# Hybrid encoder layer on one core: prompt's attention output stored in DRAM, sample's w_out low parts on VectorE, norms spread through the first MLP's end, two projection chunks multiplied beside each other

## The chip, the cores and the metric

One core of a Trainium2 chip runs the whole kernel. The metric is the device time of one execution in microseconds; less is better. The kernel before has a median of 1564.66 us over 3 runs (1561.09 to 1566.85).

Five engines work beside each other: TensorE (PE in the profile, with PEld for its weight loads), VectorE (DVE), ScalarE (ACT), GpSimd (POOL) and SyncE (SP), which here issues the transfers between DRAM and the on-chip memory. Matmul results land in eight banks of 128 x 512 fp32, which DVE and ACT read.

## The reference, cut to what matters

Two requests go through the same layer with the same weights: prompt (512 rows) and sample (1024 rows), each of width 1024.

```
h = RMSNorm(x);  z = h @ w_in                   # q 512, k 128, v 128, ca 512, cb 512 columns
A = windowed attention(q, k, v): 8 heads, 2 kv heads, |q-k| <= 128, bias per head, sink logit
B = ca * sigmoid(cb) -> depthwise conv over 31 rows -> LayerNorm over the 512 channels -> silu
x = x + concat(A, B) @ w_out
u = depthwise conv over 3 rows (RMSNorm(x) @ w_up)      # 2 x 2816 columns
x = x + (silu(u[:, :2816]) * u[:, 2816:]) @ w_down
y = RMSNorm(x)
```

All is fp32. Nearly every product is made of three matmuls on operands that are split in two: the high part (`hi`, a cast to the type fp32r, on ACT) and the low part (`lo` = value - hi, a subtraction on POOL or DVE); hi*hi, hi*lo and lo*hi are summed in a bank.

## The kernel before

**Stages.** Rows come in blocks of 128 (prompt 4, sample 8) and in groups of 512 (`nt` 0 for prompt, 1 and 2 for sample). The work goes in this order:

1. *Front.* Prompt's four x tiles are loaded and normed (`norm_in_place`, L241: sum of squares on ACT for even tiles and on DVE for odd ones, then `rstd_of`, L175, with two POOL instructions: scale and EPS at L176, power -0.5 at L177; scaling on DVE, L250). `transposed` (L254) turns them on TensorE into eight pieces of 128 x 512; ACT writes the high part (L260), DVE the low one (L261).
2. *Projection of prompt.* w_in comes in chunks of 128 columns (`order`, 14 for prompt: cb and ca of four channel groups, then k, v and four q; then the same in another order for sample). `want_raw` loads a chunk two ahead, `want_w` splits it one ahead (`split`, L189: cast L192 on ACT, subtraction L193 on POOL, or on DVE if asked). `step` (L445) multiplies one chunk with one group of rows and evacuates the bank. For the first two chunks `proj` makes the products with the weight's low part last. `constants` loads and turns small vectors after the first chunk.
3. *Projection of sample, with prompt's rest at its side.* While sample's chunks are multiplied (the loop behind `side.append(prompt())`), the generator `prompt` is advanced beside them: attention of its eight units (block x kv head), with the norm of the conv branch (`conv_norm`, L678) of a block behind each of the last four units; then, for each half n of w_out's columns, its eight pieces are loaded and split, and four out halves are made (`out_half`, L716: 24 matmuls, residual add L731, and after the second half the sum of squares L737 and its root). Then `make_h2` scales the rows and turns them for the MLP.
4. *First MLP (prompt), 22 steps, with sample's rest at its side* (`ffn_step`; L299 to L302 are the matmuls of `proj`; the three taps of the MLP's conv are L856 on ACT and L852 on DVE). From step U0 = 2 the generator `sample` gives attention for 16 units, then the 16 pieces of w_out, each loaded WOA = 5 pieces ahead and split (all low parts on POOL, since DW2 = 0), then what is left of the conv taps, and NE = 2 conv norms. The rest of sample's norms and out halves follows between this MLP and the next.
5. *Second MLP (sample)*, in an order written out by hand on TensorE, and the down projection of all rows, then `finish` (L1466) block by block: squares on ACT L1471, POOL L1472, L1473 and the power L1474, scaling on DVE L1484, store.

**What sets the order.** Within a stage the program's order is a list of generators. `tick` (L277), called every few matmuls, advances the queues by credits: `rate` for `side` (RA, RB, RBO, RD, RN, RE by stage), `conv` and `late` for the conv taps of prompt and sample (`convs`, `late`; CA, CB, CL, CLO, CD). A conv of one channel group is 31 taps; most are DVE's L354 on a bank, the last NOFF are a scaling on ACT and an add on POOL. `behind` places each tap's priority BACK places later for the scheduler, which then settles each engine's instruction order from the dependences and these priorities. Each engine and each queue works through its own list in order; SP's list holds all loads and stores.

**Buffers.** SBUF slots are taken and freed by name of size (q 4096 bytes, h 2048, c, d, s); a tile gives its slot back when the last reference goes. Banks: a (3), u (2), b (2), c (1); `use` says which job may take which. Sample's attention output (two tiles of 4 x 128 per block, high and low part) goes to DRAM (`catd`, 8 blocks, L661) and is loaded back in `load_cat` (L673). Prompt's stays on the chip from `values` until `out_half`.

## Time and profile before

| | us |
|---|---|
| median of 3 runs | 1564.66 (1561.09 to 1566.85) |
| profiled execution, its own time | 1561.29 |
| span of its trace | 1559.5 |
| PE busy | 1505.8 (97%) |
| DVE busy | 1126.9 (72%) |
| ACT busy | 795.2 (51%) |
| POOL busy | 709.7 (46%) |
| mean granted TensorE clock | 0.99 |
| matmuls and transposes in the trace | 6843 |

The profile shows one execution. Its page gives busy time of each engine, the span in 40 equal slices (39 us each; a digit is tenths of the slice), DMA queues, the chain that ended last, and groups of instructions by line. A busy PE is not PE at its peak: matmul ends are modelled, and at a lower granted clock the same matmul counts for longer. Further views used: busy time of each engine in chosen stretches, the list of what an engine waited for, the timeline, and the groups with shapes kept apart (shape out<-in, count | busy, mean ns of one | idle time ahead and what ended it).

### The profile page before, as it was taken

How to read it: one execution, taken by the hardware profiler on the slowest of the kernel's cores; microseconds unless marked ns; L12 is line 12 of the kernel's file. 1: busy time of each engine (PE TensorE's matmuls, PEld its weight loads, DVE VectorE, ACT ScalarE, POOL GpSimd, SP SyncE). 2: the span in 40 equal slices, each digit the busy share in tenths (PEclk: the TensorE clock that was granted, in tenths of full speed). 3: DMA queues.
4: the chain of work that ended last, by engine and by line, in shares of the span. 5: the costliest groups of instructions: out<-in, count | busy, mean ns of one | idle time of the engine just before them, and what ended most of it. 6: DMA issues, size and time to landing. Idle time of an engine off the chain costs nothing. (4 is left out here: it accounts for less than half of the span.)

```text
span 1559.5 us, 20112 instructions
## 1 busy us (share of the span) xinstructions
PE 1505.8 (97%) x6843; PEld 1228.9 (79%) x6843; DVE 1126.9 (72%) x1604; ACT 795.2 (51%) x1404; POOL 709.7 (46%) x566
## 2 busy tenths in 40 slices
PE   8998998899999999899999999999999999999997
PEld 6787787787888888777777888888888788888885
DVE  7999767858789785334868777777776845569883
ACT  4634654335787786623455445554545543444354
POOL 6652343226666775947434555555544000003355
PEclk9999999899999999999999999999999999999999
DMA  7582334447344346779332333333332582357644
GB/s 229 157 212 78 108 99 124 128 131 226 111 132 130 117 130 182 241 235 305 108 95 75 102 101 102 102 102 102 102 115 75 191 280 82 105 166 233 220 132 162
DMA packets 228780, 227.17 MB, mean 146 GB/s; under 512 B 13268, under 2 KB 168348, under 8 KB 228549
## 3 DMA queue, kind: packets, MB, share of 16 engines
q1 hardware_dynamic: 228677, 225.88, 45.6%
q8 instruction: 54, 0.88, 0.2%
q14 instruction: 49, 0.40, 0.1%
HBM read 164.74 MB, written 62.14 MB: 145 GB/s over the span
## 5 line engine op out<-in xcount | busy, mean ns | idle before, releaser
L193 POOL TENSOR_TENSOR q<-q,q 128x1024 fp32r<-128x1024 f32 x72 | 173.3, 2414 | 93.5 <-ACT q L192 36.7
L955 POOL TENSOR_TENSOR q<-q,q 128x512 fp32r<-128x512 f32 x101 | 140.7, 1398 | 163.8 <-ACT q L1065 151.5
L955 DVE TENSOR_TENSOR h<-h,h 128x512 fp32r<-128x512 f32 (+2 forms) x202 | 158.4, 817 | 66.2 <-ACT h L959 26.1
L1413 PE MATMUL w<-h,h 128*128 128x512 f32 x462 | 181.4, 393 | 0.5 <-DVE q L1200 0.5
L1414 PE MATMUL w<-h,h 128*128 128x512 f32 x462 | 181.5, 393 | 0.0
L1415 PE MATMUL w<-h,h 128*128 128x512 f32 x462 | 181.1, 392 | 0.0
L1079 PE MATMUL w<-h,q 128*128 128x512 f32 x448 | 176.4, 394 | 3.0 <-ACT w L1171 1.6
L1081 PE MATMUL w<-h,q 128*128 128x512 f32 x448 | 175.5, 392 | 1.0 <-POOL q L955 1.0
L1080 PE MATMUL w<-h,q 128*128 128x512 f32 x426 | 166.5, 391 | 0.0
L299 PE MATMUL u<-h,q 128*128 128x512 f32 x400 | 161.1, 403 | 5.0 <-DVE h L852 4.2
L300 PE MATMUL u<-h,q 128*128 128x512 f32 x400 | 158.9, 398 | 0.0
L302 PE MATMUL u<-h,q 128*128 128x512 f32 x384 | 152.2, 396 | 2.7 <-POOL q L193 2.7
L952 POOL TENSOR_TENSOR q<-q,q 128x1024 f32<-128x1024 f32 x12 | 33.1, 2769 | 238.1 <-DMA h<-gb 197.4
L354 DVE SCALAR_TENSOR_TENSOR c<-c,cvw,c 128x512 f32<-128x512 f32 x184 | 137.9, 750 | 2.9
L959 ACT CAST h<-h 128x512 fp32r<-128x512 f32 x120 | 71.8, 619 | 95.9 <-DVE h L955 42.5
L299 PE MATMUL b<-h,q 128*128 128x512 f32 x256 | 102.3, 400 | 2.7 <-DVE d L384 1.9
L1413 PEld LDWEIGHTS w<-h,h 128*128 128x128 f32 x462 | 86.8, 188 | 20.7 <-ACT h L959 0.9
L1415 PEld LDWEIGHTS w<-h,h 128*128 128x128 f32 x462 | 86.7, 188 | 19.7
L852 DVE SCALAR_TENSOR_TENSOR h<-u,fw,h 128x511 f32<-128x511 f32 x88 | 65.4, 744 | 50.8 <-ACT h L856 50.1
L1414 PEld LDWEIGHTS w<-h,h 128*128 128x128 f32 x462 | 86.8, 188 | 19.4
L1079 PEld LDWEIGHTS w<-h,q 128*128 128x128 f32 x448 | 84.2, 188 | 22.5 <-ACT w L1171 2.1
L302 PE MATMUL b<-h,q 128*128 128x512 f32 x256 | 101.3, 396 | 0.0
(417 smaller groups left out, 3680.3 us busy)
## 6 DMA issues: line engine op xcount, KB each, us to landing
q<-in_w_up SPq DMA_DIRECT2D x88, 512.0 KB
ga<-q SPq DMA_DIRECT2D x64, 256.0 KB
h<-ga SPq DMA_DIRECT2D x57, 256.0 KB
q<-in_w_in SPq DMA_DIRECT2D x28, 512.0 KB
h<-in_w_down SPq DMA_DIRECT2D x52, 256.0 KB
q<-in_x_sample SPq DMA_DIRECT2D x15, 512.0 KB
h<-qsd SPq DMA_DIRECT2D x24, 256.0 KB
x1d<-q SPq DMA_DIRECT2D x11, 512.0 KB
```

The costliest lines, as they stand in the source:

```text
L193: (nc.vector if dve else nc.gpsimd).tensor_tensor(lo[:], raw[:], hi[:].bitcast(F32), op=ALU.subtract)
L299: nc.tensor.matmul(out, whi[:, kc, :], hi[:], start=(kc == 0), stop=False)
L300: nc.tensor.matmul(out, whi[:, kc, :], lo[:], start=False, stop=False)
L302: nc.tensor.matmul(out, wlo[:, kc, :], hi[:], start=False, stop=(kc == KC - 1))
L354: nc.vector.scalar_tensor_tensor(acc[:], src(t), w(t), acc[:], op0=ALU.mult, op1=ALU.add)
L955: (eng or nc.vector).tensor_tensor(out, a, b, op=ALU.subtract)
L1079: nc.tensor.matmul(out, whi[:, s], hi[:], start=(start and c == 0), stop=False, **go)
L1080: nc.tensor.matmul(out, whi[:, s], lo[:], start=False, stop=False, **go)
L1081: nc.tensor.matmul(out, wlo[:, s], hi[:], start=False, stop=(stop and c == 3), **go)
L1413: nc.tensor.matmul(out, sh[:, c], th[:], start=(p == 0), stop=False)
L1414: nc.tensor.matmul(out, sh[:, c], tl[:], start=False, stop=False)
L1415: nc.tensor.matmul(out, sl[:, c], th[:], start=False, stop=(p == NPAIR - 1))
```

## The change

- *Prompt's attention output* is stored to DRAM too (`catd` grows to 12 blocks: eight stores of 256 KB more) and loaded back by `conv_norm` (eight loads more).
- *Prompt's generator* makes all attention units first, without norms between; then conv norms 0 and 1, the first half of w_out, out half (0,0), out half (1,0) alternating with the loads and splits of w_out's second half (`beside`), out halves (0,1) and (1,1) alternating with conv norms 2 and 3, then (2,1), (3,1), (2,0), (3,0), then `make_h2`. `halves_done` counts halves, since the second column half may now come first.
- *Sample's w_out*: the low parts of all 16 pieces on DVE (DW2 = 4; `m % 4 < DW2`). After the first WON = 6 pieces the others alternate with what is left of the taps and the NE conv norms; the two attention outputs are asked for earlier (m = 2, 4 in place of 10, 12).
- *First two chunks* of w_in: their high parts are cast on ACT ahead of the transposed x's, their low parts on POOL behind the root of the fourth x tile; `first_two` multiplies piece by piece of x with both chunks' high parts, then both with the low parts, and `constants` comes behind them.
- *Norms*: for odd x tiles DVE's reduction takes in the scale and EPS, so one POOL instruction of the two goes; `finish` scales in the square and needs one POOL instruction less per block.
- *Pacing constants* RB, RBO, RN, CA, CL, CLO, CD and BACK change; the front's turns may use bank c.

TensorE's instructions are 6844 in both programs; DVE's list goes from 1606 to 1622, POOL's from 571 to 537, SP's from 827 to 843.

```diff
-RA, RB, RBO, RD, RN, RE = 1.2, 0.8, 2.5, 0.8, 0.95, 0.9
+RA, RB, RBO, RD, RN, RE = 1.2, 0.7, 0.6, 0.8, 1.15, 0.9
-CA, CB = 0.9, 0.4
-CL, CLO, CD = 0.6, 1.0, 0.6
+CA, CB = 0.85, 0.4
+CL, CLO, CD = 0.55, 0.9, 0.66
-WOP, WOA, DW, DW2 = 1, 5, 2, 0
+WOP, WOA, DW, DW2 = 1, 5, 2, 4
+WON = 6
-BACK = (200, 1500)
+BACK = (200, 600)
...
     def norm_in_place(x, k):
...
-            nc.vector.tensor_tensor_reduce(out=junk[:], in0=x[:], in1=x[:], scale=1.0, scalar=0.0,
+            nc.vector.tensor_tensor_reduce(out=junk[:], in0=x[:], in1=x[:], scale=1.0 / D, scalar=EPS,
                                            op0=ALU.mult, op1=ALU.add, accum_out=ss[:])
-        rstd_of(ss[:], D, rs[:])
+        if k % 2 == 0:
+            root = rstd_of(ss[:], D, rs[:])
+        else:
+            root = nc.gpsimd.tensor_tensor(rs[:], ss[:], nhalf[:], op=ALU.pow)
+        marks.append(root.ins)
...
+    def first_two():
+        pp = [bank("step") for _ in range(2)]
+        for kc in range(KC):
+            hi, lo = h1[0][kc]
+            for i in range(2):
+                whi = ws[i][0]
+                nc.tensor.matmul(pp[i][:], whi[:, kc, :], hi[:], start=(kc == 0), stop=False)
+                nc.tensor.matmul(pp[i][:], whi[:, kc, :], lo[:], start=False, stop=False)
+            if kc % 2 == 1:
+                tick()
+        for i in range(2):
+            for kc in range(KC):
+                nc.tensor.matmul(pp[i][:], ws[i][1][:, kc, :], h1[0][kc][0][:], start=False, stop=(kc == KC - 1))
+            kind, c, _ = order[i]
+            evac(kind, c, 0, pp[i][:])
...
     want_raw(1)
-    for _ in make_h1(0):
+    use.update(turn="aubc")
+    for k, x in enumerate(xq[0]):
+        norm_in_place(x, k)
+    his = []
+    for i in range(2):
+        hi = sb.tile([KC, P], F32R)
+        nc.scalar.copy(hi[:], raws[i][:])
+        his.append(hi)
+    h1[0] = []
+    for _ in transposed(xq.pop(0), gA, h1[0]):
         pass
-    with tc.issue_after(marks[0][0]):
-        want_w(0)
+    use.update(turn="aub")
+    with tc.issue_after(marks[3]):
+        for i in range(2):
+            lo = sb.tile([KC, P], F32R)
+            nc.gpsimd.tensor_tensor(lo[:], raws.pop(i)[:], his[i][:].bitcast(F32), op=ALU.subtract)
+            ws[i] = his[i], lo
...
-    with tc.issue_after(marks[KC - 1][0]):
-        want_w(1)
...
-        if kv == 1 and G["g"] == 1:
+        if kv == 1:
             cats.pop((i, 0))
             for L in range(2):
-                nc.sync.dma_start(catd[b, :, L, :].rearrange("p (j t) -> p j t", t=P), cat[L][:].bitcast(F32))
+                nc.sync.dma_start(catd[i, :, L, :].rearrange("p (j t) -> p j t", t=P), cat[L][:].bitcast(F32))
...
-        if G["g"] == 1 and (i, 0) not in cats:
+        if (i, 0) not in cats:
             load_cat(i)
...
-        if n == 1:
+        halves_done[i] = halves_done.get(i, 0) + 1
+        if halves_done[i] == 2:
...
+    def beside(gen, other):
+
+        for _ in gen:
+            yield 0.0
+            if next(other, None) is not None:
+                yield 0.0
+        yield from other
...
     def prompt():
-        yield from attention(0, 8, {u: conv_norm(u - 4) for u in range(4, 8)})
+        yield from attention(0, 8)
         kt.clear(), vt.clear(), qt.clear(), bias.clear()
         pace.update(rate=RBO, late=CLO)
...
+        for i in range(2):
+            yield from conv_norm(i)
+        yield from w_half(0)
+        yield from out_half(0, 0)
+        yield from beside(out_half(1, 0), w_half(1))
+        for i, n in ((0, 1), (1, 1)):
+            yield from beside(out_half(i, n), conv_norm(i + 2))
+        for n in (1, 0):
+            for i in (2, 3):
                 yield from out_half(i, n)
-            wo.clear()
+            for kc in range(KC):
+                wo.pop((kc, n))
         yield from make_h2(0, 0)
...
+    def wo_pieces():
+        for m in range(16 + WOA):
+            if m in (2, 4):
+                load_cat(m // 2 + 3)
+            if m < 16:
+                load_wo(m // 2, m % 2)
+            if m >= WOA:
+                split_wo((m - WOA) // 2, m % 2, m % 4 < DW2)
+                yield 0.0
+
+    def norms():
+        drain(late)
+        for m in range(NE):
+            yield from conv_norm(4 + m)
+
     def sample():
...
-        for m in range(16 + WOA):
-            if m in (10, 12):
-                load_cat(m // 2 - 1)
-            if m < 16:
-                load_wo(m // 2, m % 2)
-            if m >= WOA:
-                split_wo((m - WOA) // 2, m % 2, m % 4 < DW2)
-                yield 0.0
-        drain(late)
-        for m in range(NE):
-            yield from conv_norm(4 + m)
+        wos = wo_pieces()
+        for _ in range(WON):
+            next(wos)
+            yield 0.0
+        yield from beside(wos, norms())
...
     def finish(blk, parts, tail):
...
-            nc.scalar.activation(o[:, s], parts[n], AF.Square, accum_out=ss[:, n:n + 1])
-        nc.gpsimd.tensor_scalar(rs[:, 0:1], ss[:, 0:1], 1.0 / D, EPS, op0=ALU.mult, op1=ALU.add)
-        nc.gpsimd.tensor_scalar(rs[:, 1:2], ss[:, 1:2], 1.0 / D, rs[:, 0:1], op0=ALU.mult, op1=ALU.add)
+            nc.scalar.activation(o[:, s], parts[n], AF.Square, scale=D ** -0.5, accum_out=ss[:, n:n + 1])
+        nc.gpsimd.tensor_scalar(rs[:, 1:2], ss[:, 1:2], ss[:, 0:1], EPS, op0=ALU.add, op1=ALU.add)
         nc.gpsimd.tensor_tensor(rs[:, 1:2], rs[:, 1:2], nhalf[:], op=ALU.pow)
```

More of the change, by code (lines that the diff above doesn't have):

```diff
@@ L176, in rstd_of @@
         nc.gpsimd.tensor_scalar(out, ss, 1.0 / n, EPS, op0=ALU.mult, op1=ALU.add)
-        nc.gpsimd.tensor_tensor(out, out, nhalf[:], op=ALU.pow)
+        return nc.gpsimd.tensor_tensor(out, out, nhalf[:], op=ALU.pow)
     def load_x(G, tt):
@@ L203, in tile_hybrid_encoder @@
     nch = len(order)
-    raws, ws = {}, {}
+    raws, ws, asked = {}, {}, set()
     def want_raw(i):
-        if i < nch and i not in raws and i not in ws:
+        if i < nch and i not in raws and i not in ws and i not in asked:
+            asked.add(i)
             raws[i] = chunk_raw(w_in[0], order[i][2])
     def want_w(i):
-        if i < nch and i not in ws:
+        if 1 < i < nch and i not in ws:
             want_raw(i)
@@ L263, in transposed @@
             h.append((hi, lo))
[L264 removed]
+            last.append((ia.ins, iv.ins))
             yield 0.0
@@ L293, in drain, with proj @@
             advance(queue)
-    def proj(out, w, h, late_lo=False):
+    def proj(out, w, h):
         whi, wlo = w
@@ L300, in proj @@
             nc.tensor.matmul(out, whi[:, kc, :], lo[:], start=False, stop=False)
-            if not late_lo:
-                nc.tensor.matmul(out, wlo[:, kc, :], hi[:], start=False, stop=(kc == KC - 1))
+            nc.tensor.matmul(out, wlo[:, kc, :], hi[:], start=False, stop=(kc == KC - 1))
             if kc % 2 == 1 and kc < KC - 1:
                 tick()
-        for kc in range(KC if late_lo else 0):
-            nc.tensor.matmul(out, wlo[:, kc, :], h[kc][0][:], start=False, stop=(kc == KC - 1))
     qsd = [dr.tile([4, P, NH, P], F32, name=f"qsd{i}") for i in range(3)]
@@ L311, in tile_hybrid_encoder @@
     ksd = dr.tile([HD, NKV, 2, 1024], F32, name="ksd")
-    catd = dr.tile([8, P, 2, 4 * P], F32, name="catd")
+    catd = dr.tile([12, P, 2, 4 * P], F32, name="catd")
     cvd = [dr.tile([P, 4, G["T"]], F32, name=f"cvd{G['g']}") for G in GR]
@@ L435, in make_h1 @@
             if nt == 1:
-                with tc.issue_after(marks[KC - 1][0]), tc.issue_after(marks[KC - 1][1]):
+                with tc.issue_after(last[KC - 1][0]), tc.issue_after(last[KC - 1][1]):
                     norm_in_place(x, k)
@@ L511, in tile_hybrid_encoder @@
             bbd = bias_to_dram()
+        if i == 0:
+            first_two()
         want_raw(i + 2)
         want_w(i + 1)
-        step(i, 0)
-        ws.pop(i)
+        if i > 1:
+            step(i, 0)
+            ws.pop(i)
     drain(side)
@@ L675, in load_cat @@
         for L in range(2):
-            nc.sync.dma_start(cats[i, 0][L][:].bitcast(F32), catd[blocks[i][1], :, L, :].rearrange("p (j t) -> p j t", t=P))
+            nc.sync.dma_start(cats[i, 0][L][:].bitcast(F32), catd[i, :, L, :].rearrange("p (j t) -> p j t", t=P))
     def conv_norm(i):
```

22 lines of the change are left out of this document (12 added, 10 removed).

## The prediction, made before the result was known

> **What bounds the kernel now.** The page's first two parts come first: which engine is full, and in which slices it isn't.
>
> ```profile
> PE 1505.8 (97%) x6843; PEld 1228.9 (79%) x6843; DVE 1126.9 (72%) x1604; ACT 795.2 (51%) x1404; POOL 709.7 (46%) x566
> ...
> PE   8998998899999999899999999999999999999997
> ...
> DVE  7999767858789785334868777777776845569883
> ...
> PEclk9999999899999999999999999999999999999999
> ```
>
> TensorE (PE) is the bound. The change leaves its instructions as they are, 6844 in both orders, so only its idle time and its granted clock can be won or lost. Idle time sits in the first eighth of the span, where VectorE (DVE) reads 9 several times, and at slices 17 to 19. The busy time by stretches puts sizes on it; the columns are the stretch, its length, then PE, weight load, DVE, ACT and POOL busy, the clock, the DMA share and GB/s.
>
> ```profile
> 40.00:80.00 40.00, 36.13 (x188) 29.24 (x187) 39.43 (x56) 24.56 (x37) 26.85 (x24) 1.00 0.52 155
> 120.00:160.00 40.00, 35.55 (x166) 28.84 (x167) 36.24 (x80) 20.18 (x53) 9.51 (x7) 0.96 0.27 80
> 160.00:200.00 40.00, 37.31 (x184) 30.63 (x183) 31.96 (x69) 26.98 (x61) 16.83 (x12) 1.00 0.29 89
> 254.00:284.00 30.00, 21.16 (x89) 16.46 (x88) 17.46 (x28) 14.64 (x28) 14.13 (x14) 0.83 0.45 131
> 360.00:400.00 40.00, 38.50 (x189) 31.64 (x188) 32.99 (x67) 24.76 (x46) 25.71 (x16) 1.00 0.56 175
> 640.00:662.00 22.00, 17.83 (x67) 13.82 (x66) 6.58 (x9) 11.28 (x18) 21.84 (x15) 0.84 0.73 242
> 662.00:760.00 98.00, 92.82 (x436) 75.05 (x435) 47.15 (x71) 30.27 (x60) 56.53 (x80) 1.00 0.74 247
> 900.00:940.00 40.00, 40.00 (x176) 32.62 (x175) 30.85 (x30) 19.55 (x29) 21.27 (x15) 1.00 0.31 101
> ```
>
> The last row is a stretch without loss: 40/176 = 0.227 us for a 512-column matmul. I count a stretch's loss as (length - PE busy) + length x (1 - clock), since a matmul at half clock still reads as busy. That gives: first projection chunks (40:80) 3.9; prompt's attention (120:200) 4.45 + 1.6 + 2.7 = 8.7; prompt's layer norms (254:284) 8.8 + 5.1 = 13.9; start of the first MLP (360:400) 1.5; the end of that MLP (640:760) 4.2 + 3.5 + 5.2 = 12.9. **41 us in all**, the most that the parts before 760 us can give. The list of what TensorE waited for (total, times, longest) names the causes:
>
> ```profile
> PE u L299 <- DVE h L852: 4.2, 2, 3.5
> PE u L702 <- DVE q L696: 4.0, 1, 4.0
> PE u L702 <- DVE h L696: 3.0, 1, 3.0
> ...
> PE u L726 <- DVE s L693: 2.2, 1, 2.2
> ...
> PE a L575 <- DVE s L582: 1.8, 1, 1.8
> ...
> PE a L690 <- DMA h<-cvd: 1.6, 2, 1.0
> ```
>
> L696 is the layer norm of the conv branch, L582 the scores' reduction, L852 the MLP's three taps. The two L696 waits, 7 us, are the 254:284 stretch.
>
> **The change part by part.** Durations of the instructions that it moves (count | busy, mean ns | idle before):
>
> ```profile
> L193 POOL TENSOR_TENSOR q<-q,q 128x1024 fp32r<-128x1024 f32 x72 | 173.3, 2414 | 93.5 <-ACT q L192 36.7 <-issue 28.0 <-DMA qsd<-q 11.0
> ...
> L354 DVE SCALAR_TENSOR_TENSOR c<-c,cvw,c 128x512 f32<-128x512 f32 x184 | 137.9, 750 | 2.9
> ...
> L852 DVE SCALAR_TENSOR_TENSOR h<-u,fw,h 128x511 f32<-128x511 f32 x88 | 65.4, 744 | 50.8 <-ACT h L856 50.1
> ...
> L856 ACT ACTIVATE h<-u,vecs,fw 128x512 f32<-128x512 f32 x44 | 34.2, 777 | 53.8 <-PE u L302 53.4
> ...
> L193 POOL TENSOR_TENSOR h<-h,h 128x512 fp32r<-128x512 f32 x16 | 20.3, 1290 | 0.6 <-ACT h L192 0.6
> ...
> L250 DVE TENSOR_SCALAR q<-q,s 128x1024 f32<-128x1024 f32 x12 | 14.8, 1237 | 3.5 <-POOL s L177 3.4
> ...
> L261 DVE SCALAR_TENSOR_TENSOR h<-a,vecs,h 128x512 fp32r<-128x512 f32 x20 | 14.3, 742 | 4.2 <-ACT h L260 4.2
> ...
> L737 ACT ACTIVATE h<-q 128x1024 bf16<-128x1024 f32 x11 | 11.6, 1059 | 19.9 <-DVE q L731 19.6 <-DVE h L710 0.2
> ...
> L731 DVE TENSOR_TENSOR q<-u,q 128x512 f32<-128x512 f32 x17 | 11.6, 685 | 9.5 <-PE u L728 9.5
> ...
> L193 DVE TENSOR_TENSOR h<-h,h 128x512 fp32r<-128x512 f32 x12 | 8.1, 686 | 5.9 <-PE u L727 4.0 <-ACT h L192 1.6
> ...
> L696 DVE TENSOR_SCALAR h<-a,s,s 128x512 f32<-128x512 f32 x9 | 7.3, 807 | 5.4 <-POOL s L177 5.4
> ...
> L177 POOL TENSOR_TENSOR rs<-rs,nhalf 128x1 f32<-128x1 f32 x12 | 6.6, 549 | 0.7
> ...
> L176 POOL TENSOR_SCALAR rs<-s 128x1 f32<-128x1 f32 x12 | 2.7, 222 | 33.4 <-ACT h L737 32.9
> ...
> L737 ACT ACTIVATION_READ_ACCUMULATOR h<-q 128x1 f32 x11 | 2.1, 189 | 0.0
> ```
>
> 1. *First two chunks beside each other, one POOL instruction less for odd x tiles.* The timeline of the start (start, duration):
>
> ```profile
> 11.68 0.75 POOL L176 TENSOR_SCALAR s<-s 128x1 f32<-128x1 f32 x1
> ...
> 14.27 0.69 ACT L260 ACTIVATE h<-u,vecs 128x512 fp32r<-128x512 f32 x1 [4.51 <-PE u L258]
> 14.86 1.04 ACT L192 CAST q<-q 128x1024 fp32r<-128x1024 f32 x1
> 14.99 0.75 DVE L261 SCALAR_TENSOR_TENSOR h<-u,vecs,h 128x512 fp32r<-128x512 f32 x1 [1.14 <-ACT h L260]
> ```
>
> The 0.75 us at 11.68 leaves the chain of the last x tile. But two casts of 1.04 now stand ahead of the first L260 instead of one behind it, so the hi parts start about where they did. Until the low parts have all come (8 x 0.742 = 5.9 us) TensorE had 2 x 0.227 = 0.45 us of work for each; now it has 0.91, more than the 0.74. That could win 8 x (0.74 - 0.45) = 2.3 us. DVE, however, is full at 39.43 of 40 just behind (40:80), and it has no less to do by then, so most of the gain meets that limit. Bounds 0 and 2.3; I take **0.7**, nearer to the full DVE.
>
> 2. *Prompt's attention without the norms between, other pacing of the conv taps.* In 120:160 DVE is busy for 36.24, PE for 35.55: DVE is late. I multiplied the instructions in the two orders by the durations above and took the largest stretch in which DVE's work outgrows TensorE's: by 24.8 us before (TensorE's 529th to 745th instruction), by 18.7 after (503rd to 733rd), since some eight taps of 0.750 fall outside. The difference, 6.1 us, is the most that this model gives; part of the excess was covered by lead already. Bounds 0 and 8.7 (all of the loss); I take **5**. The eight new stores of prompt's attention output stand in SP's queue and wait for POOL's last add of a block; behind them are the loads of w_in chunks, asked for two chunks (four matmul groups of 24, 4 x 24 x 0.227 = 22 us) ahead. That lead covers them, so I price them at nothing; without it, one late chunk costs its wait.
>
> 3. *Prompt's norms and out-projection.* The norms' transposes and the out halves now lie between projection groups, 42 or more matmuls (9.5 us) from one norm step to the next, against a root and scaling of 0.222 + 0.549 + 0.807 and the statistics ahead of them. The eight new loads of the stored output go out with the cvd loads, 26 to 30 matmuls (6 us) ahead of the transposes; two cvd loads made TensorE wait now, 1.0 at most, so four blocks could cost 0 to 4 here; I take 0, since none of the eight is needed before the out halves. So the 13.9 us of 254:284 go. What is late next: w_in's matmuls now end at TensorE's 1400th instruction, and the last 172 before make_h2 are out halves alone. Block 3's second half ends them, and nothing is left to put into its chain: add 0.685, square 1.059 + 0.19, root 0.222 + 0.549, scaling 0.75 (1.237 in the mean) = 3.5 to 3.9 us, then transposes, L260's 0.69, and L261 behind three taps of 0.750: 6.9 us less 1.4 of TensorE's work in it, **5.5**. Up to the 1653rd instruction DVE then has 29 instructions of 0.75 in a row, 21.7 us, against 14.7 of TensorE: another 5.4. There both halves of the first MLP step end together, and two splits of 2.414 on POOL come due: 0.6 more. So 11.5 us idle. For the clock I take the 640:662 row: one wait of 3.5 us there (L852) went with 22 x 0.16 = 3.5 us lost. Two holes here give 3.5 to 7, taken at 5. The stage thus costs 16.5 after, against 13.9 + 1.5: **1 lost**, with bounds of 15.4 gained (no hole opens) and 26 lost (rival below). The Trainium skill, page "TensorE: Matmul & The Clock Gate", section "Part 1: The HAM clock gate", says that the clock halves after an idle window of about 3.4 us and returns after about as long of sustained work: by that one hole costs 1.7 us, two 3.4, and the stage would come out 1.6 us better than mine. The row's 3.5 us after one hole is twice that.
>
> 4. *w_out's low parts for the sample on VectorE, norms inside the MLP's end.* POOL loses 16 x 1.290 = 20.6 us around 640, where it is busy for 21.84 of 22; DVE gains 16 x 0.686 = 11 where it is busy for 6.58 of 22 and 47.15 of 98. So the taps' 3.5 us wait and its clock loss should go: 4.2 + 3.5 = 7.7, of which ACT's casts, late by a w_out load as before, may keep a part. Of the 5.2 in 662:760, 2.2 is L693 and 1.6 cvd loads. The new order still has three places where a transpose or out half follows the load or the cast that it needs by under 7 us of matmuls, and a norm chain covered by 0.7. Bounds 2 and 12.9; I take **6.7**.
>
> 5. *The tail.* After the last matmul the chain passes two POOL instructions ahead of the root; one goes.
>
> ```profile
> 1554.21 0.26 POOL s L1473
> ```
>
> **0.4** (0.26 and its hand-over).
>
> Sum: 0.7 + 5 - 1 + 6.7 + 0.4 = 11.8. The profiled execution took 1561.29 (span 1559.5), which gives 1549.5; it lies 0.2 above the fastest of the runs shown and 3.4 under their median of 1564.66, which stands for what a typical run takes and against which I forecast: 1564.7 - 11.8 = **1552.9**.
>
> **The rivals.**
> - *The new holes eat the gain.* If stage 3 costs 24 instead of 16.5 (DVE's backlog of taps grows by what attention left undone: 6 us) and attention gives 2, late MLP 4: 0.7 + 2 - 8.5 + 4 + 0.4 = -1.4, so 1566. For it: the taps are the same number, only later. Against: DVE is not full around that place (32.99 of 40 in 360:400).
> - *Slower: no filler.* Conv norms 2 and 3, make_h2 and the first MLP step each open a hole as wide as 254:284 (13.9 with its clock): 4 x 13.9 = 56 - 15.4 = 40 at the worst; with three of them, 26 lost, 12.8 won elsewhere, 13 net: **1578**. It decides if, at the 1400th instruction, DVE still holds over some 9 us of taps (the cover of 42 matmuls). For it: no projection matmul is left to fill in. Against: the norm steps are far apart in the order.
> - *All holes close.* 41 less some 13 remaining: 28 won, **1537**. It needs make_h2's chain to be hidden, for which the order shows no work.
> - That the change does not do what it says is excluded as far as the orders go: POOL has 34 instructions fewer, DVE 16 more, SP 16 more.
>
> **How the numbers follow.** Forecast (1545 to 1557) 0.50; all closed (1532 to 1545) 0.12; eaten (1557 to 1572) 0.23; slower (over 1572) 0.15. About 0.5% is what a measurement can tell here: under 1556.8 is faster, over 1572.5 slower. Faster: nearly all of the first two, 0.61; same 0.24; slower 0.15. The range, 1537 to 1573, leaves out the lower half of "all closed" and most of "slower", some 0.2.
>
> **What would show it.** Step 1: the third chunk's matmuls start about a microsecond earlier. Step 2: PE busy over 120:200 rises by about 4. Step 3: no wait on L696 over 1 us; instead a wait of PE's transposes on L250's scaling of 3 us or more near 360, and the clock under 1 behind it. Step 4: 640:662 without a wait on L852, POOL idle there for 10 us. Wrong would be a wait on a w_in or catd load, a hole before the out halves, or TensorE waiting on the low parts on DVE.

## The result and the profile after

| | before | after |
|---|---|---|
| median, 4 runs each beside each other | 1562.88 (1560.95 to 1566.85) | 1582.92 (1581.95 to 1583.84) |
| ratio to before, 95% interval | | 1.0132 (1.0114 to 1.0149) |
| profiled execution, its span | 1561.29, 1559.5 | 1583.06, 1581.3 |
| mean granted TensorE clock | 0.990 | 0.981 |

The change makes the kernel 1.3% slower, where 1552.9 was forecast: 30 us off, and above the range. The page of the kernel after, with the lines that answer to the prediction's first fence:

```profile
PE 1516.1 (96%) x6843; PEld 1234.2 (78%) x6843; DVE 1151.3 (73%) x1620; ACT 795.5 (50%) x1404; POOL 691.7 (44%) x532
...
PE   8999999988999999997999999999999999999995
...
DVE  7889574957599897733767787787777845568883
...
PEclk9999999998999999998999999999999999999998
```

Counted from 0, PE's 8 in slice 6 (234 to 273 us), where prompt's norms stood, is gone. Two new dents have come: slices 8 and 9 (316 to 395 us) and, deeper, slice 18 (711 to 751); the clock reads 8 in slices 9 and 18. The last slice reads 5 where it read 7.

PE's busy time alone misleads here, since it rose by 10 us: at a lower clock the same matmul counts for longer. So a stretch's **loss** is read from the starts of the matmuls: each gap to the next start, less the median gap of its shape, summed. For the prediction's rows this agrees with its own measure ((length - busy) + length x (1 - clock)) to within 2 us. By stretches, in us:

| | 0-120 | 120-250 | 250-345 | 345-400 | 638-785 | 785-900 and 1180-1265 | from the last matmul's start to the end |
|---|---|---|---|---|---|---|---|
| before | 16.0 | 10.7 | 12.8 | 1.9 | 13.9 | 8.1 | 12.0 |
| after | 14.2 | 9.0 | 0.1 | 16.0 | 28.2 | 7.7 | 17.3 |

Where the 21.8 us of span come from: the first MLP's end and the passage to the second +14.3, the tail +5.3, prompt's end and the first MLP's start +1.4, the front and attention -3.5, the two quiet stretches -0.4. That leaves 4.7, taken up at the end. The windows of the kernel after that stand for these stretches (columns as in the prediction):

```profile
120.00:160.00 40.00, 39.38 (x194) 32.38 (x192) 37.90 (x76) 22.85 (x54) 11.48 (x8) 1.00 0.37 99
160.00:200.00 40.00, 37.25 (x165) 30.85 (x166) 22.97 (x48) 24.07 (x51) 15.01 (x10) 0.91 0.28 92
254.00:284.00 30.00, 30.00 (x139) 24.63 (x138) 18.27 (x27) 14.49 (x28) 10.90 (x10) 1.00 0.82 243
345.00:390.00 45.00, 35.79 (x144) 27.86 (x144) 33.24 (x53) 20.04 (x31) 19.89 (x14) 0.81 0.37 117
640.00:662.00 22.00, 18.95 (x72) 14.78 (x71) 15.55 (x18) 11.84 (x17) 14.74 (x8) 0.84 0.69 209
638.00:785.00 147.00, 128.90 (x564) 102.54 (x563) 76.72 (x110) 53.39 (x101) 67.48 (x85) 0.93 0.64 207
```

and the last of them in the kernel before:

```profile
638.00:785.00 147.00, 137.65 (x631) 111.08 (x630) 73.68 (x107) 55.25 (x106) 92.23 (x105) 0.98 0.65 214
```

254:284 is full at a clock of 1.00, and 345:390 now has 9.2 us without a matmul and a clock of 0.81. In 638:785 TensorE does 564 matmuls and transposes where it did 631, with 24.7 us *less* work on POOL. What TensorE waited for longest in the kernel after (total, times, longest):

```profile
PE b L1069 <- DVE q L1040: 5.8, 2, 5.4
PE a L266 <- DVE q L818: 4.3, 2, 3.3
PE u L307 <- ACT q L193: 4.1, 1, 4.1
PE a L687 <- DVE h L675: 3.0, 1, 3.0
PE c L767 <- ACT h L750: 2.7, 1, 2.7
...
PE c L768 <- DVE h L194: 2.1, 1, 2.1
```

L818 is the scaling in `make_h2` and L193 the cast of a w_up chunk: prompt's two holes. L1069 turns sample's scaled rows (L1040) between the MLPs; L767 and L768 are out-half matmuls: L767 waits for the high part of the normed conv branch, a cast on ACT (L750), and L768 for w_out's low part, now a subtraction on DVE (L194). In the kernel before, the turn that answers to L1069 waited far less:

```profile
PE b L1002 <- DVE q L973: 0.6, 1, 0.6
```

No wait on conv_norm's scaling (L737 now) is above 1.1.

### The profile page after: what moved, and what is told of

Same layout as the page of the kernel before. It is cut to its first block, busy times and chain, and to the rows that moved or that the text cites. A ratio compares the mean times of both kernels' runs of the same rounds, so it can differ in the third digit from the quotient of the medians.

```text
span 1581.3 us, 20147 instructions
## 1 busy us (share of the span) xinstructions
PE 1516.1 (96%) x6843; PEld 1234.2 (78%) x6843; DVE 1151.3 (73%) x1620; ACT 795.5 (50%) x1404; POOL 691.7 (44%) x532
## 5 line engine op out<-in xcount | busy, mean ns | idle before, releaser
L194 POOL TENSOR_TENSOR q<-q,q 128x1024 fp32r<-128x1024 f32 x70 | 169.8, 2431 | 132.0 <-ACT q L193 73.8
L1022 DVE TENSOR_TENSOR h<-h,h 128x512 fp32r<-128x512 f32 (+2 forms) x206 | 161.7, 818 | 66.9 <-DMA h<-in_w_down 24.8
L1022 POOL TENSOR_TENSOR q<-q,q 128x512 fp32r<-128x512 f32 x81 | 112.7, 1403 | 160.2 <-ACT q L1132 155.3
L307 PE MATMUL u<-h,q 128*128 128x512 f32 x384 | 156.3, 408 | 5.7 <-ACT q L193 4.1
L308 PE MATMUL u<-h,q 128*128 128x512 f32 x384 | 154.0, 401 | 0.0
L309 PE MATMUL u<-h,q 128*128 128x512 f32 x384 | 154.0, 401 | 0.0
L1146 PE MATMUL w<-h,q 128*128 128x512 f32 x368 | 145.2, 394 | 2.5 <-ACT h L1229 1.8
L1148 PE MATMUL w<-h,q 128*128 128x512 f32 x368 | 144.5, 393 | 0.6 <-POOL q L1022 0.6
L1147 PE MATMUL w<-h,q 128*128 128x512 f32 x346 | 135.9, 393 | 0.0
L1019 POOL TENSOR_TENSOR q<-q,q 128x1024 f32<-128x1024 f32 x9 | 24.4, 2722 | 250.0 <-DMA h<-gb 197.9
L307 PE MATMUL b<-h,q 128*128 128x512 f32 x256 | 103.1, 403 | 1.8 <-DVE h L394 1.8
L309 PE MATMUL b<-h,q 128*128 128x512 f32 x256 | 101.5, 396 | 0.0
L308 PE MATMUL b<-h,q 128*128 128x512 f32 x256 | 101.2, 395 | 0.0
L352 POOL TENSOR_TENSOR h<-h,h 128x512 f32<-128x512 f32 x59 | 77.7, 1316 | 51.2 <-ACT h L351 41.1
```

The lines of the kernel that those rows point to most:

```text
L194: (nc.vector if dve else nc.gpsimd).tensor_tensor(lo[:], raw[:], hi[:].bitcast(F32), op=ALU.subtract)
L307: nc.tensor.matmul(out, whi[:, kc, :], hi[:], start=(kc == 0), stop=False)
L308: nc.tensor.matmul(out, whi[:, kc, :], lo[:], start=False, stop=False)
L309: nc.tensor.matmul(out, wlo[:, kc, :], hi[:], start=False, stop=(kc == KC - 1))
L1022: (eng or nc.vector).tensor_tensor(out, a, b, op=ALU.subtract)
L1146: nc.tensor.matmul(out, whi[:, s], hi[:], start=(start and c == 0), stop=False, **go)
```

## Experiments

One theory put the late loss on the changed sequence of `sample` with its low parts on DVE (step 4's own content). Its rivals were the pacing constants, which the prediction had costed at nothing, and the memory slots. Each table below gives medians, the ratio to before with its interval, and losses in stretches of 0-250, 250-400, 638-785 and the tail. The losses come from one profile each. The two quiet stretches scatter over 7 to 11 us in the 18 profiles, and the kernel before and b1, which differ only at the end, differ by 1.4 and 1.8 in 250-400 and 638-785. So losses that differ by less than 3 us are read as equal.

**Tail: the lost slot.** The front's loop now stands in the function itself, so the name `x` keeps the last prompt tile, and its slot of 4096 bytes, to the end. *a1* lets go of it.

```diff
-    hi = lo = None
+    hi = lo = x = None
```

> The changed kernel plus one thing: the Python name x that the new front leaves behind is cleared, so that the last input tile of prompt gives its 4096-byte slot back after the front (15 such slots in use again instead of 14). Theory M (memory): the lost slot makes the last output tiles rotate through two buffers instead of three, each waiting for a store of two blocks before; the time from the last matmul to the end goes from 17.3 back to 12.0 us, and the total falls by 5 us (1578). If the missing slot also delays loads and tiles between 640 and 780 us, the total falls by up to 15. Rival: only the tail moves, and the 28 us that TensorE loses between 640 and 780 stay.

*a2* needs no output tile: results are written over the bank's copy and stored from there; *b1* does the same in the kernel before.

```diff
-        ss, o = early[tt] = sm(2), sb.tile([D])
+        ss, o = early[tt] = sm(2), sb.tile([D], BF16, 2)
...
-                nc.scalar.activation(o[:, s], parts[n], AF.Identity, scale=rs[:, 1:2])
+                nc.scalar.activation(parts[n], parts[n], AF.Identity, scale=rs[:, 1:2])
...
-            nc.sync.dma_start(G["o"][b * P:(b + 1) * P, s], o[:, s])
+            nc.sync.dma_start(G["o"][b * P:(b + 1) * P, s], parts[n])
```

> The changed kernel with its final outputs written into the sums' own tiles, and the squares' unused result in a 2048-byte tile; the lost slot stays lost. Theory M: the tail needs no output buffer, so ACT's waits for out_sample and out_prompt stores (3.3 us each) go and the tail falls from 17.3 to 12 us or less: total 1577 to 1578, and nothing before 1540 us moves. If the tail is bound by POOL's multiplications (2 x 1.5 us) instead, it falls by less than 2 us.

> The kernel before with its final outputs written into the sums' own tiles, as in a2. Theory M (the tail waits for output buffers): the last matmul stays at 1547.5 us, the time behind it falls from 12.0 us to the 7.3 us of a2, total 1558 to 1560. Rival: with three buffers the tail is bound by POOL and DVE, and falls by under 1 us. Its matmul pitch also shows whether the 0.2305 to 0.2310 us between matmuls of all changed kernels, against 0.2301 before, is the kernel or the chip of that profile.

| | median | ratio | 0-250 | 250-400 | 638-785 | tail |
|---|---|---|---|---|---|---|
| before | | | 26.7 | 14.7 | 13.9 | 12.0 |
| after | 1582.92 | 1.0132 (1.0114 to 1.0149) | 23.2 | 16.1 | 28.2 | 17.3 |
| a1_free_x | 1580.84 | 1.0110 (1.0091 to 1.0129) | 23.7 | 16.7 | 28.9 | 11.4 |
| a2_out_in_place | 1573.40 | 1.0059 (1.0042 to 1.0076) | 22.2 | 16.4 | 27.7 | 7.3 |
| b1_before_inplace | 1558.88 | 0.9968 (0.9951 to 0.9984) | 26.8 | 16.1 | 15.7 | 7.3 |

The slot sets the tail. Timeline of ACT at the end of the kernel after:

```profile
1564.10 0.63 ACT L1538 ACTIVATE q<-q 128x512 f32<-128x512 f32 x1 [3.33 <-DMA out_prompt<-q]
...
1572.29 0.63 ACT L1530 ACTIVATE q<-q 128x512 f32<-128x512 f32 x1 [3.31 <-DMA out_sample<-q]
```

and the corresponding rows of the kernel before:

```profile
1545.03 0.63 ACT L1471 ACTIVATE q<-q 128x512 f32<-128x512 f32 x1 [3.32 <-DMA out_prompt<-q]
...
1547.43 0.63 ACT L1463 ACTIVATE q<-q 128x512 f32<-128x512 f32 x1 [1.06 <-POOL s L1474]
```

The last blocks' output tiles take turns in three slots before and in two after, so the squares, whose discarded results go into the output tile, wait for a *store* to land. With three slots that happens too, 2.5 us ahead of the last matmul's start (3.32 at 1545.03); with two it also holds up the very last block (3.31 at 1572.29). With the slot back the tail is 11.4, with no output tile 7.3 in either kernel. The slot did not hurt the MLP: a1's 638-785 reads 28.9. That removes the memory rival for the larger loss. Of a1's 5.9 us in the tail only 2.1 show in the medians, 3.4 by the two ratios; its last matmul starts 3.1 us later than after's, without a cause that I can name.

**The late loss: sequence, low parts or pacing.** *a3* puts the low parts back on POOL (DW2 = 0). *a4* has the body of `sample` of before, DW2 = 0, RN = 0.95, CD = 0.6. *b3* has that body with DW2 = 4 and the new RN = 1.15, CD = 0.66; *c2* that body with DW2 = 0 and the new RN and CD. *c1* is the kernel after with only RN and CD put back, *d1* with only RN, *d2* with only CD.

```diff
-RA, RB, RBO, RD, RN, RE = 1.2, 0.7, 0.6, 0.8, 1.15, 0.9
+RA, RB, RBO, RD, RN, RE = 1.2, 0.7, 0.6, 0.8, 0.95, 0.9
```

> The changed kernel with the low parts of sample's w_out on POOL again (DW2 = 0), all else as changed. Theory D: the 16 subtractions on DVE, which took up to 2.65 us instead of 0.69 while POOL ran its own splits, hold up the out halves (TensorE waited 2.1 us for one) and the taps; without them 640 to 662 loses less than its 6.2 us, total 2 to 6 less. Rival: POOL gets 20.6 us of work back and its queue, which holds the norms' roots, gets longer: total the same or up to 8 more.

> The changed kernel with the sample's part as before: all 16 pieces of w_out split on POOL ahead of the remaining taps and the two norms, loads of the attention output at pieces 10 and 12, RN 0.95, CD 0.6. Theory S: the 14 us that 640 to 780 lost against before lie in the new sequence; total 12 to 16 less (1567 to 1571). Theory M: they lie in the lost slot; then TensorE's loss between 640 and 780 stays near 28 us and the total moves by under 4.

> The changed kernel with the sample's pieces, taps and norms in the old sequence, but DW2 = 4 and the changed RN and CD. Theory S (the sequence): TensorE's loss in 662 to 785 goes from 22 to about 8 us as in a4, while 638 to 662 stays at 6 or more because of the DVE low parts; total about 1569 to 1573. Rival P (pacing RN and CD): the loss stays near 20 us, total 1580.

> The changed kernel with the old sequence and DW2 = 0, but RN 1.15 and CD 0.66 as changed. Theory P (pacing): the loss in 638 to 785 stays above 21 us (b3's 30.3 less the 5.5 that DW2 brought), total 1576 to 1580. Rival D (the low parts on DVE made b3 slow): near a4's 15.5, total 1571 to 1573.

> The changed kernel with two pacing constants back, RN 0.95 and CD 0.6; sequence and DVE low parts (DW2 = 4) as changed. So far TensorE's loss in 638 to 785 us is 28.2 as changed, 22.7 with DW2 = 0, 30.3 with the old sequence alone, 15.5 with all three back. Theory P (pacing): about 20 here, total 1573 to 1576. Rival S (it takes sequence and pacing together): about 28, total 1581 to 1584.

> The changed kernel with RN back to 0.95 and CD as changed (0.66). Theory R: RN decides, since it sets when w_out's pieces and the two norms are put between the MLP's matmuls: loss in 638 to 785 about 12 us as in c1, total 1570 to 1573. Theory T (taps): CD decides, loss stays at 22 or more, total 1579 to 1584.

> The changed kernel with CD back to 0.6 and RN as changed (1.15). Theory R: loss in 638 to 785 stays at 22 or more, total 1579 to 1584. Theory T: about 12 us, total 1570 to 1573. If both single steps give about 12, each alone moves the order out of the bad place.

| | RN | body of `sample`, DW2 | median | ratio | 638-785 |
|---|---|---|---|---|---|
| after | 1.15 | new, 4 | 1582.92 | 1.0132 (1.0114 to 1.0149) | 28.2 |
| a3_dw2_0 | 1.15 | new, 0 | 1576.99 | 1.0083 (1.0063 to 1.0102) | 22.7 |
| b3_seq_old_dw2 | 1.15 | old, 4 | 1586.52 | 1.0139 (1.0122 to 1.0156) | 30.3 |
| c2_seq_dw2 | 1.15 | old, 0 | 1591.88 | 1.0158 (1.0128 to 1.0187) | 36.5 |
| d2_cd_only | 1.15 | new, 4 | 1581.65 | 1.0102 (1.0075 to 1.0129) | 26.4 |
| a4_sample_old | 0.95 | old, 0 | 1571.97 | 1.0053 (1.0037 to 1.0069) | 15.5 |
| c1_pace_only | 0.95 | new, 4 | 1571.18 | 1.0040 (1.0026 to 1.0053) | 12.3 |
| d1_rn_only | 0.95 | new, 4 | 1572.57 | 1.0046 (1.0031 to 1.0061) | 14.5 |

My theory fell. Whatever the sequence and the engine of the low parts, the loss in this table is 22.7 to 36.5 with RN = 1.15 and 12.3 to 15.5 with RN = 0.95. **One number in a line of constants is the cause**: d1, which changes nothing else, wins back 13.7 of the 14.3 (10.4 in the medians), and CD alone does not. The window in d1:

```profile
638.00:785.00 147.00, 138.99 (x626) 111.34 (x625) 89.92 (x123) 57.13 (x106) 79.43 (x91) 0.97 0.69 223
```

626 matmuls against 564. RN is the credit per tick for the generator `sample` in its last part, so 1.15 takes the out halves and the turns between the MLPs earlier in the order. The first turn of sample's rows (L1069, L1002 in the kernel before) stands at 709.5 us after and 711.8 in d2, against 737.0 before, 732.9 in d1 and 734.8 in c1. There it is ahead of its inputs. The POOL timeline of the kernel after:

```profile
686.67 0.74 POOL L951 TENSOR_TENSOR h<-h,h 128x256 f32<-128x256 f32 x1 [9.85 <-DMA h<-gt]
...
704.91 0.75 POOL L952 TENSOR_TENSOR h<-h 128x256 f32<-128x256 f32 x1 [7.63 <-DMA h<-gt]
...
710.59 0.72 POOL L953 TENSOR_TENSOR h<-h,h 128x256 f32<-128x256 f32 x1
711.39 0.19 POOL L177 TENSOR_SCALAR rs<-s 128x1 f32<-128x1 f32 x1
...
713.29 0.55 POOL L178 TENSOR_TENSOR rs<-rs,nhalf 128x1 f32<-128x1 f32 x1
```

the DVE instruction that needs this root:

```profile
713.88 1.28 DVE L1040 SCALAR_TENSOR_TENSOR q<-q,rs,q 128x1024 f32<-128x1024 f32 x1 [7.96 <-POOL rs L178]
715.08 0.81 DVE L737 TENSOR_SCALAR h<-a,s,s 128x512 f32<-128x512 f32 x1
```

and TensorE:

```profile
715.22 0.69 PE L1069 MATMUL b<-ident,q 128*128 128x128 f32 x2 [5.38 <-DVE q L1040]
```

Read backwards: TensorE waits 5.4 for a scaled block, DVE 8.0 for its root, and the root stands on POOL behind a row of the MLP's pair sums (L951 to L954), the first of which (704.91) waited 7.6 for a load. The next conv norm's scaling (L737) stands behind L1040, and its own root behind the same row. In d1 no L1069 waits in this window, and the longest of POOL's waits on those loads is 3.6. Behind this wait the clock reads 0.50 for 10.24 us, which costs 5.1 more:

```profile
714.77:725.01 10.24, 7.06 (x20) 5.03 (x21) 4.07 (x7) 3.81 (x8) 5.28 (x8) 0.50 0.89 292
```

The wait and its clock, 10.5 us, are most of the 14.3. The profiles put the loss in the same place: 700 to 726 us loses 10.1 to 13.9 in all eight kernels with RN = 1.15, and 1.0 to 7.1 in the ten with 0.95. What is late there differs, though. In b3 and c2 it is a load of the attention output, in a3 a load of the conv's output; here are their longest waits between 700 and 726, in this order:

```profile
PE u L767 <- DMA h<-catd: 6.8, 1, 6.8
PE u L767 <- DMA h<-catd: 5.1, 1, 5.1
PE a L731 <- DMA h<-cvd: 6.6, 2, 5.3
```

That RN causes the loss is shown, and so is its place; that it goes through the chain above in the kernel after is read from the trace and was not tried by itself.

**The low parts on DVE.** The lines of w_out's low part by source, DVE, 632 to 680 us, in the kernel after (minimum, median, maximum ns):

```profile
L194 DVE TENSOR_TENSOR h<-h,h x16: 657/693/2652, 632.0 to 679.8; 128x512 fp32r<-128x512 f32 x16
```

The median is close to the prediction's 686, but seven took 770 to 2652. The timelines of POOL and of DVE show what ran beside:

```profile
645.57 4.71 POOL L194 TENSOR_TENSOR q<-q,q 128x1024 fp32r<-128x1024 f32 x2 [6.05 <-ACT q L193]
650.23 1.74 POOL L940 TENSOR_TENSOR h<-h,h 128x512 f32<-128x512 f32 x1
...
655.18 2.73 POOL L194 TENSOR_TENSOR q<-q,q 128x1024 fp32r<-128x1024 f32 x1
```

```profile
648.18 4.34 DVE L194 TENSOR_TENSOR h<-h,h 128x512 fp32r<-128x512 f32 x2 [0.44 <-ACT h L193]
...
656.30 0.73 DVE L910 SCALAR_TENSOR_TENSOR h<-u,fw,h 128x511 f32<-128x511 f32 x1
```

Two low parts took 4.34 us beside a POOL split of two SBUF operands, where 1.39 was to be expected, and POOL's product of the gate (L940), 1.30 elsewhere, took 1.74. All seven slow low parts had a POOL instruction that reads SBUF beside them; the other nine took 657 to 693. A tap (L910) that reads one operand from a bank took its usual 0.73 inside the next such split, and so did the others: 37 taps inside a POOL split have a median of 0.745, as have the 51 elsewhere. The Trainium skill, page "GPSIMD Engine Reference", section "1. Specifications", says that GpSimd shares its SBUF interface with VectorE and names VectorE instructions with two SBUF inputs among those that contend; the rows agree, and they give the size, a factor of up to 3.8. In time it is worth little: a3 at RN = 1.15 gains 5.5 us in 638-785 by going back to POOL, but with the old sequence (c2 against b3) the sign is the other way.

**Prompt's order.** *b5* puts `prompt` and its constants back (RB 0.8, RBO 2.5, CA 0.9, CL 0.6, CLO 1.0, BACK 1500). *c3* is the kernel before with the new front, the norms' arithmetic and the slot freed. *b7* is c3 with outputs in place and YN = 4, the beats between a conv norm's scaling and its second turns (2 in both kernels). *c4* is the kernel before with outputs in place, four beats for prompt alone, and RBO = 5:

```diff
-RA, RB, RBO, RD, RN, RE = 1.2, 0.8, 2.5, 0.8, 0.95, 0.9
+RA, RB, RBO, RD, RN, RE = 1.2, 0.8, 5.0, 0.8, 0.95, 0.9
...
 YN = 2
+YP = 4
...
-        for _ in range(YN):
+        for _ in range(YP if G["g"] == 0 else YN):
```

> The changed kernel with prompt's part as before: norms within the attention, both halves of w_out in turn, no store of prompt's attention output, old RB, RBO, CA, CL, CLO, BACK. The trace says that prompt's part traded one hole for another: TensorE's loss in 250 to 345 goes from 0 back to about 13 us, that in 345 to 400 from 16 to about 2, total within 4 us of the changed kernel. Rival: the new order gains in the attention as I had forecast (5 us); then this is 3 to 7 slower.

> The kernel before with the new front (two chunks beside each other), the new norms' and finish's arithmetic, and x cleared; prompt's and sample's parts as before. By my forecast the front is worth 0.7 and the finish 0.4: total 1 to 3 under before. TensorE's loss in 0 to 120 us is 16.0 before and 11.8 to 14.2 in the changed kernels, so 2 to 4 here. If the longer matmul pitch (0.2310 against 0.2301 us) comes with the front, the total is the same as before.

> Old prompt and sample parts with the new front and the new norms' arithmetic, outputs in place as in a2, x cleared as in a1, and YN = 4 in place of 2, so that two more projection steps lie between a conv norm's statistics and its second turn. If the front gains 2 to 3, the tail 5, and the longer distance closes the 13 us hole of 250 to 345, the total is 1542 to 1547; if DVE is late there whatever the distance, the hole stays and the total is 1555.

> The kernel before with outputs in place (as in b1) and two numbers changed for prompt: four advances of the queue instead of two between a conv norm's statistics and its second turn, and RBO 5 instead of 2.5, so that the out halves end while projection matmuls are left. Theory F (filler): a hole opens wherever a chain of prompt's has no projection matmul beside it, so this closes both: loss in 250 to 345 from 12.8 to under 2, in 345 to 400 under 4, total 1558.9 - 11 = 1546 to 1550. Rival: the hole moves on again, as in the changed kernel and in b7; then 345 to 400 loses 12 or more and the total stays above 1556.

| | median | ratio | 0-120 | 120-250 | 250-345 | 345-400 | 638-785 | tail |
|---|---|---|---|---|---|---|---|---|
| b5_prompt_old | 1579.24 | 1.0086 (1.0065 to 1.0107) | 14.2 | 6.9 | 10.0 | 5.0 | 27.6 | 17.4 |
| c3_front_only | 1565.43 | 1.0006 (0.9989 to 1.0023) | 15.7 | 5.5 | 10.7 | 8.2 | 15.9 | 11.6 |
| b7_best_yn4 | 1566.83 | 1.0009 (0.9995 to 1.0023) | 14.6 | 5.4 | 0.1 | 15.8 | 25.4 | 7.3 |
| c4_both_holes | 1550.45 | 0.9900 (0.9872 to 0.9929) | 16.6 | 12.6 | 0.0 | 4.5 | 15.6 | 7.3 |

The new order moves prompt's hole, it does not close it: 10.0 + 5.0 with the old order (b5), 0.1 + 16.0 with the new. b7 shows the same hand-over with the *old* order once the norm's chain is given more distance. There, as I read the trace, the hole opens where the sample's projection matmuls have run out and prompt's last block is still under way. c4 gives the chain distance and credit enough to end in time, and both holes go:

```profile
250.00:345.00 95.00, 95.00 (x430) 77.82 (x429) 62.08 (x91) 41.64 (x77) 27.20 (x26) 1.00 0.45 131
345.00:400.00 55.00, 51.73 (x251) 42.18 (x251) 48.73 (x94) 32.08 (x60) 34.05 (x23) 1.00 0.62 186
```

against the second of these stretches in the kernel after:

```profile
345.00:400.00 55.00, 45.79 (x193) 36.31 (x193) 38.50 (x73) 25.50 (x45) 22.09 (x16) 0.84 0.32 101
```

b7 and d3 (below) tell part of what does it. Both have the new front, the old order and four beats for prompt; they differ in RBO (2.5 and 5) and in sample's beats, which come into play only behind 600 us. 250-400 loses 15.9 in b7 and 5.6 in d3, so the distance alone moves the hole, and it takes the credit as well to close it. Whether the credit alone would do, and either with the new order of prompt, was not tried. b7 also gives sample four beats, and its late loss is 25.4, so there the longer distance hurts.

The attention's gain is the front's: with the new front the fourteen profiles other than after's read 20.0 to 25.2 in 0-250, with either order of prompt, against 26.7, 26.8 and 29.2 with the old front. c3, with the old order, has 21.2. In 120-250 alone the new order even costs: the ten profiles that have it read 8.3 to 12.0, the five with the new front and the old order 5.4 to 6.9.

**The parts that pay, together.** *d3* is c4 with the new front, the norms' arithmetic and the slot freed; *d4* adds the new body of `sample` with DW2 = 4, at RN = 0.95 and CD = 0.6.

> c4 (outputs in place, both holes of prompt closed) with the new front and the new norms' arithmetic, x cleared. If the front's 2 us are kept: 1547 to 1550; if the longer matmul pitch comes with it (3 to 4 us), 1550 to 1553.

> d3 with the changed sample part too (w_out's low parts on DVE, pieces beside norms) at the old pacing RN 0.95, CD 0.6. My step 4 said that this part wins 6.7 us; c1 has 12.3 us of loss in 638 to 785 against 13.9 before, so 1.6: total 1 to 2 under d3. Rival: the low parts on DVE beside POOL's splits cost 5 us as in a3: total 3 to 5 over d3.

| | median | ratio | 0-250 | 250-400 | 638-785 | tail |
|---|---|---|---|---|---|---|
| d3_front_holes | 1551.70 | 0.9915 (0.9890 to 0.9940) | 24.8 | 5.6 | 18.8 | 7.4 |
| d4_front_holes_sample | 1546.93 | 0.9880 (0.9858 to 0.9902) | 24.5 | 5.9 | 15.8 | 7.4 |

**d4 beats both kernels.** With the old RN the new `sample` is worth about 3 us of loss, and 4.8 in the medians; the times of d3 (1550.9 to 1555.4) and d4 (1546.2 to 1548.2) do not overlap, though their intervals do. The front adds nothing on top of c4 (1550.45 against 1551.70): 0-250 gains 4.4 (29.2 to 24.8), and 250-400 and 638-785 give 1.1 and 3.2 of it back, besides the wider pitch of matmuls described at the end of the next section.

## Why the prediction was wrong, step by step

1. *Front, +0.7.* Sized low at the third chunk, and its bound was in the wrong place. The third chunk starts at 28.62 us where it started at 31.56, 2.9 us earlier, above the 2.3 that I gave as an end; 0-120 lost 16.0 and loses 14.2. So by 120 us 1.8 are left (0.3 in c3), less than I can tell from nothing; most of what the front gains shows in the next stretch.
2. *Attention, +5.* Busy time over 120:200 rose by 3.8, as asked for, but the clock fell to 0.91 in 160:200, which costs 3.6; 120-250 gains 1.7. Steps 1 and 2 together gained 3.5 of 5.7. The reason was wrong: with the front alone (c3) the stretch gains 5.2, and with the new order too it gains less. The front does it, and not the order of the norms with its constants, which was to free DVE (that the front does so by letting DVE start its taps earlier is likely, and was not tried by itself); the new stores and loads appear in no wait of TensorE.
3. *Prompt's norms and out-projection, -1.* Right in place, and in size partly by luck: 250-400 goes from 14.7 to 16.1. The two holes came where the order was said to run out, one at make_h2's scaling (3.3, forecast 5.5), one ahead of the first MLP step (4.1, forecast 5.4 + 0.6; the working shown for the 5.4, 21.7 - 14.7, gives 7.0). The timeline of TensorE in the kernel after:

```profile
355.40 0.90 PE L266 MATMUL a<-ident,q 128*128 128x128 f32 x3 [3.28 <-DVE q L818]
```

```profile
378.51 0.76 PE L307 MATMUL u<-h,q 128*128 128x512 f32 x1 [4.14 <-ACT q L193]
```

   The second hole did not come from DVE's backlog of taps. The cast on ACT that it waits for had itself waited for a load of w_up, and SyncE had issued these loads late, behind a transpose of make_h2 (L266) and a matmul of the step before (L309); that these two held the slots is my reading. The timeline of ACT and the waits of SP from 340 to 380 us:

```profile
377.41 1.04 ACT L193 CAST q<-q 128x1024 fp32r<-128x1024 f32 x1 [1.14 <-DMA q<-in_w_up]
```

```profile
SPq L187 <- PE a L266: 14.8, 1, 14.8
...
SPq L187 <- PE u L309: 4.3, 1, 4.3
```

   Less idle time than forecast (9.2 us in 345:390, against 11.5) met a dearer clock: 45 x 0.19 = 8.6 us, above the 5 that I took and the 3.5 to 7 that I bounded. The windows show where it went, a low stretch behind each hole and the 3.4 us ahead of it:

```profile
349.54:352.96 3.42, 1.58 (x8) 0.81 (x6) 2.64 (x3) 1.41 (x2) 3.03 (x3) 1.00 0.37 117
352.96:363.20 10.24, 7.02 (x21) 5.11 (x22) 9.52 (x14) 4.17 (x8) 3.10 (x3) 0.50 0.20 78
373.44:376.85 3.41, 0.93 (x5) 0.59 (x4) 1.93 (x3) 2.39 (x3) 3.04 (x2) 1.00 0.65 191
376.85:383.68 6.83, 5.17 (x12) 4.12 (x13) 6.76 (x16) 3.13 (x6) 5.20 (x3) 0.50 0.32 96
```

   The estimate that the prediction worked out from the Trainium skill ("TensorE: Matmul & The Clock Gate", "Part 1: The HAM clock gate"), 1.7 us for a hole, gives 3.4 for these two. The low stretches measured here are three and two times 3.41 us, and the first began when no idle gap had yet lasted over 1.1 us.
4. *Sample's low parts and the MLP's end, +6.7 with bounds of 2 and 12.9.* **The step that failed: it came out at -14.3.** Step 4 read the order of TensorE around 640:662, and there the change did about what was said: the wait on the taps fell from 3.5 to 1.0 (now L307 on L910) and PE busy went from 17.83 to 18.95, while low parts on DVE at up to 2.65 us in place of 0.686 and the new wait on them (L768, 2.1) kept the loss of 638 to 662 at 6.2 (7.1 before); POOL was idle there for 7.3 us, where 10 had been named. But RN was priced at nothing by not being named. It moved the turns between the MLPs 28 us forward (737.0 to 709.5), a place that the two orders show before any run, and none of step 4's terms covers it. The three places where a transpose or out half follows its load or cast by under 7 us were noted and given no price of their own. With RN at 0.95 the step is worth 3 to 5 us in d4, inside its bounds, but 1.6 in c1 and nothing in d1 (14.5), which have prompt's new order; differences of this size are within the scatter.
5. *Tail, +0.4.* Came out at -5.3. The instruction did go, and with the slot back (a1) the tail is 0.6 shorter than before; the price of a slot held by a name was not seen, since only the instructions of the chain were counted and not the buffers that the last output tiles rotate through.

What is left, 4.7 us, no step has. Some 3 of it are a slightly wider pitch of matmuls where nothing waits. The stretch 1260:1540 in the kernel after:

```profile
1260.00:1540.00 280.00, 280.00 (x1214) 227.67 (x1213) 187.66 (x233) 112.27 (x194) 45.59 (x24) 1.00 0.53 177
```

and in the kernel before:

```profile
1260.00:1540.00 280.00, 280.00 (x1217) 228.23 (x1216) 185.29 (x230) 114.02 (x208) 59.27 (x46) 1.00 0.50 165
```

and in c3:

```profile
1260.00:1540.00 280.00, 280.00 (x1213) 227.71 (x1213) 187.00 (x231) 111.60 (x200) 55.77 (x32) 1.00 0.52 170
```

280/1214 against 280/1217 is 0.25%, and over some 1300 us 3 us. The wider pitch goes with the new front: over this stretch the three kernels with the old front (before, b1, c4) have 1217, 1217 and 1219 matmuls, the fifteen with the new one 1210 to 1215. It comes with c3, which has the front, the norms' arithmetic and the slot alone, and c3's total is level with the kernel before, as was expected for that case. Why the front widens the pitch stays open.

Of the rivals, none named the mechanism. The one that ended slower (1578, no filler at prompt's end) came nearest in time, but its place reads 1.4 us; the time went by a wait in another stage.

## What to carry to other kernels

A constant that sets how fast one list is taken against another is a change of order like any other: write down where each wait's producer and consumer stand under the new value, and price the places where they come closer, before costing it at nothing. A hole that is moved is paid for where the filler ends; look for the distance *and* the credit that let the chain end before the filler does. Where a kernel manages its memory by references, count the slots behind a change at the end of the kernel too: there a store's landing, not an engine, can set the time.

## What the runs showed of the hardware

- A DVE subtraction of 128x512 with both operands in SBUF takes 0.69 us alone and up to 2.65 us beside a POOL subtraction of 128x1024, while the tap with an operand in a bank keeps its 0.73. POOL's product of 128x512 goes from 1.30 to 1.74 there.
- The clock falls to 0.50 without one long wait. It changes in steps of 3.41 us. Cut into such steps, the 18 traces from 25 to 1540 us show 83 falls, each behind a step in which TensorE had been busy for 1.98 us or less; of the 6995 steps behind which it stayed up, none had less than 1.54. In one of the falls the longest single gap of the step ahead was 0.62 us. It then stayed low for 3.41, 6.83, 10.24 or 13.65 us. So short waits that fall close together cost clock as one long wait does: in the kernel after, 8.6 us for two holes of 3.3 and 4.1 us.
- With two output slots in place of three, ACT waits 3.3 us for a store to land twice in the last 20 us, where it did so once.
